# Weight loads from GpSimd's DMA queue, stores of the prepared scan features from ScalarE's

## The chip, the core and the metric

The kernel runs on one core of one Trainium2 chip. The metric is the device time of one execution in microseconds, as the median of three runs. The core has a matrix engine (PE; PEld is its weight load), three engines for elementwise work (DVE is VectorE, ACT is ScalarE, POOL is GpSimd) and SP (SyncE), which here does nothing but issue DMAs. Each engine works through its own list of instructions strictly in order, and an instruction that has to wait, a DMA issue too, holds up everything behind it in that list.

## The reference, cut to what matters

One layer of a diffusion backbone on 1024 latent and 128 context tokens (T = 1152 columns), D = 1024, all float32:

```python
h = rmsnorm(x, norm1_g) * (1 + sc1) + sh1
z = h @ w_in                                   # r, k, v, low-rank decay/rate/gate, conv branch, gates
o_a = rwkv_mixer(r, k, v, ...)                 # 16 heads, forward and backward scan over the tokens
o_b = cb * seq_conv(cc * cx, ...)
merged = g_a * (o_a @ w_pa) + g_b * (o_b @ w_pb)
x = x + gt1 * (merged @ w_o)
u = seq_conv(rmsnorm(x, norm2_g) * ... @ w_up, ...)
x = x + gt2 * ((silu(u_act) * u_lin) @ w_down)
y = rmsnorm(x, norm_f_g)
```

## The kernel before, in words

Tokens lie along the free dimension in three column blocks of 384. A *job* is one 128-row output tile of one weight matrix: 8 row blocks of the contraction, three column blocks, and three matmuls for each (the operands are split into a rounded high part and the rest, and hi·hi, hi·lo and lo·hi are summed), so 72 matmuls of 384 columns. `dense` (L230 on) is a generator over the jobs. A job's weights come as two halves of 128 x 4 x 128 values (256 KB): `load_w` (L197 on) starts the DMA into a buffer `wraw` (two buffers), `split_w` (L212 on) rounds it on ACT into `whi` and subtracts on another engine into `wlo` (three buffers each). The first half for the next job is loaded when a job begins and split after its first column block; the second half is loaded there and split later in the job. The subtraction runs on POOL while the scan is going on and on DVE afterwards. The small matrix `g2` goes through `load_w` as well, and there the matmuls read `wraw` itself.

From about 75 us to 1800 us the jobs of `w_in` and `w_pb` are interleaved with the scan, which runs as a set of generators (class `Scan`):

- `prep` (L1106 on), for each of 8 head pairs and 3 column blocks and both directions: loads `krk` and, through `lora_in`, `llo`, makes the scan features `fa` and `ak` on ACT and DVE, and stores them to DRAM (`FA`, `FB`, L1179), and once per block the bonus product `bt` to `BS` (L1167).
- `features` (L1190 on), for each of 36 scan items: loads `E`, `O` (out of `FA`) and `BK` (out of `FB`); then `prep2` makes the Gram products `gpb`, `gpk` on PE.
- `to_blocks`, `chain_load`, `chain`: the diagonal blocks go to DRAM (`Dd`) and come back as `Dm`, loaded from POOL's queue; 62 small DVE operations (`Xt`, `X`) invert them; the result is stored (`Xd`) from ACT's queue.
- `vfill`, `merge`, `scan`, `finish`: value tiles `Wt`, the scan's own matmuls, and the normalised output, which loads `fv`, `fg` and (out of `BS`) `fb`.

After 1800 us come the projections `w_pa` and `w_o`, then the feed-forward part (`w_up`, `w_down`) to the end. The program gives every operation a priority in the order in which the generators emit it; the framework makes from that, at compile time, one fixed list for each engine. Buffers that are reused put semaphore waits into those lists. Every DMA goes through one function:

```python
q = {"S": self.nc.sync, "A": self.nc.scalar, "G": self.nc.gpsimd}[QUEUE.get(kind, "S")]
q.dma_start(out=out, in_=in_)
```

`kind` is a name that the caller gives. `load_w` gives "w", the `bt` store "bs", and both feature stores "fa". The weights of the last down projection and all that has no kind go to SP.

Of the kernel before, what the change touches and what calls it, by code (L numbers as in the profile page):

```python
# [31 lines left out]

T_R, T_K, T_V, T_WD, T_AD, T_GD, T_CB, T_CC, T_CX, T_GA, T_GB = 0, 8, 16, 24, 25, 26, 27, 35, 43, 51, 59

QUEUE = dict(Xw="A", Dm="G")

PCOLS = {}
_n = 0
# [38 lines left out]
class Kern:  # L77
# [47 lines left out]
    def dma(self, out, in_, kind=None):  # L125

        q = {"S": self.nc.sync, "A": self.nc.scalar, "G": self.nc.gpsimd}[QUEUE.get(kind, "S")]
        q.dma_start(out=out, in_=in_)  # L128
# [1404 lines left out]
```

## Time and profile before

| | |
|---|---|
| median of 3 runs | 3000.38 us (2999.66 to 3003.8) |
| profiled execution | 2994.76 us, span of the profile 2993.0 us |
| PE | busy 2771.6 us, 93% of the span |
| PEld | 84% of the span |
| DVE | 2009.7 us, 67% |
| ACT | 1266.4 us, 42% |
| POOL | 318.9 us, 11% |
| DMA packets' share of 16 engines | q1 39.6%, q0 2.3%, q10 1.0% |

Busy time of PE is read as presence: matmuls overlap, and a busy PE is not one at its peak. SP has no busy time; its issues are seen in the timeline and in the view of a tile. q1 is the queue of the DMAs that SP issues, q0 that of POOL, q10 that of ACT. Where a wait is for several things, the view names what came last.

### The profile page before, as it was taken

Reading aid. Unit: us, or ns where it says so; the run is one execution under the profiler, and the core shown is the slowest. Engines: PE = TensorE matmul, PEld = TensorE weight load, DVE = VectorE, ACT = ScalarE, POOL = GpSimd, SP = SyncE. Lnnn points to the kernel's source line nnn. Section 1 sums busy time; section 2 is a strip of 40 time slices with the busy share of each in tenths; the row PEclk is TensorE's granted clock in tenths of the full one; section 3 lists DMA queues with packets and bytes.
Section 4 is the critical chain, followed back from the end, with each engine's and each line's share of the span. In section 5 each row is a group of like instructions: output and inputs, shape, how many; then the busy total and the mean of one; then the engine's idle time right before and its main releaser. Section 6 shows DMA issues by size and latency. Waiting matters only on the chain. (4 is left out here: it accounts for less than half of the span.)

```text
span 2993.0 us, 63336 instructions
## 1 busy us (share of the span) xinstructions
PE 2771.6 (93%) x24762; PEld 2514.2 (84%) x24762; DVE 2009.7 (67%) x5039; ACT 1266.4 (42%) x2540; POOL 318.9 (11%) x342
## 2 busy tenths in 40 slices
PE   7886989999989988988998999899999999999997
PEld 3774778878778877777777789899999999999996
DVE  8367666677568779989877865965555454454556
ACT  5464536454545633334543544023443241424243
POOL 3211111111111111111111112100000000000001
PEclk9997999999999999999999999999999999999999
DMA  4577646464655644544554538853211111111112
GB/s 191 179 240 204 197 121 209 145 180 143 184 172 166 197 118 127 136 115 122 148 136 120 137 101 279 291 165 98 68 43 36 50 40 45 41 41 43 41 44 81
DMA packets 425937, 388.50 MB, mean 130 GB/s; under 512 B 189477, under 2 KB 362405, under 8 KB 425637
## 3 DMA queue, kind: packets, MB, share of 16 engines
q1 hardware_dynamic: 379558, 360.84, 39.6%
q0 software_dynamic: 6912, 18.88, 2.3%
q10 hardware_dynamic: 39168, 4.73, 1.0%
q8 instruction: 195, 3.19, 0.5%
q14 instruction: 104, 0.85, 0.1%
HBM read 268.17 MB, written 116.13 MB: 128 GB/s over the span
## 5 line engine op out<-in xcount | busy, mean ns | idle before, releaser
L89 PE MATMUL psd<-h,whi 128*128 128x384 f32 x3216 | 909.3, 355 | 20.4 <-ACT h L105 9.3
L89 PEld LDWEIGHTS psd<-h,whi 128*128 128x128 f32 x3216 | 592.3, 192 | 58.6 <-issue 12.6
L89 PE MATMUL psd<-h,wlo 128*128 128x384 f32 x1608 | 564.5, 352 | 3.6 <-POOL wlo L110 3.6
L89 PE MATMUL psd<-g,whi 128*128 128x384 f32 (+1 forms) x2112 | 543.2, 338 | 0.0
L105 ACT ACTIVATE whi<-wraw 128x512 fp32r<-128x512 f32 (+2 forms) x334 | 198.4, 595 | 457.5 <-PE psd L89 358.6
L89 PEld LDWEIGHTS psd<-g,whi 128*128 128x128 f32 x2112 | 383.5, 188 | 0.3
L89 PE MATMUL psd<-g,wlo 128*128 128x384 f32 (+1 forms) x1056 | 355.9, 337 | 0.0
L110 POOL TENSOR_TENSOR wlo<-wraw,whi 128x512 fp32r<-128x512 f32 x148 | 207.1, 1402 | 1208.6 <-ACT whi L105 1057.4
L89 PEld LDWEIGHTS psd<-h,wlo 128*128 128x128 f32 x1608 | 309.3, 192 | 17.3 <-POOL wlo L110 5.2
L110 DVE TENSOR_TENSOR X<-X,Xt 128x60 f32<-128x60 f32 (+24 forms) x1116 | 258.0, 233 | 27.3
L110 DVE TENSOR_TENSOR Xt<-X,Dm 128x60 f32<-128x60 f32 (+24 forms) x1116 | 257.4, 233 | 27.0
L89 PE MATMUL psd<-a,whi 128*128 128x384 f32 x864 | 219.0, 334 | 0.0
L89 PE MATMUL psd<-x,whi 128*128 128x384 f32 x768 | 199.7, 341 | 8.0 <-ACT x L105 4.4
L89 PEld LDWEIGHTS psd<-g,wlo 128*128 128x128 f32 x1056 | 199.3, 189 | 0.0
L110 DVE TENSOR_TENSOR wlo<-wraw,whi 128x512 fp32r<-128x512 f32 (+2 forms) x186 | 113.7, 612 | 102.9 <-ACT whi L105 102.9
L89 PEld LDWEIGHTS psd<-a,whi 128*128 128x128 f32 x864 | 156.0, 188 | 0.0
L110 DVE TENSOR_TENSOR fu<-psd,rs 128x384 f32<-128x384 f32 x132 | 73.4, 556 | 117.3 <-PE psd L89 105.2
L89 PEld LDWEIGHTS psd<-x,whi 128*128 128x128 f32 x768 | 140.6, 191 | 10.3 <-ACT x L105 4.7
L89 PE MATMUL psd<-a,wlo 128*128 128x384 f32 x432 | 144.0, 334 | 0.0
L122 DVE SCALAR_TENSOR_TENSOR x<-psd,mod,x 128x384 f32<-128x384 f32 (+3 forms) x160 | 79.2, 515 | 93.9 <-PE psd L89 93.8
L105 ACT ACTIVATE BK<-BK,PC 128x128 f32<-128x128 f32 x288 | 93.2, 392 | 102.2 <-PE gpk L89 77.9
L89 PE MATMUL psd<-x,wlo 128*128 128x384 f32 x384 | 130.5, 340 | 5.4 <-DVE wlo L110 5.4
(206 smaller groups left out, 4917.7 us busy)
## 6 DMA issues: line engine op xcount, KB each, us to landing
wraw<-in_w_in SPq DMA_DIRECT2D x134, 256.0 KB, 3.2
wraw<-in_w_up SPq DMA_DIRECT2D x88, 256.0 KB, 2.6
llo<-lo SPq DMA_DIRECT2D x98, 192.0 KB, 2.7
BK<-fb SPq DMA_DIRECT2D x36, 512.0 KB, 4.8
Dm<-Dd POOLq DMA_DIRECT2D x144, 128.0 KB, 3.6
wx<-in_wmb SPq DMA_DIRECT2D x32, 512.0 KB, 5.3
fa<-fa SPq DMA_DIRECT2D x40, 384.0 KB, 2.7
fb<-ak SPq DMA_DIRECT2D x40, 384.0 KB, 3.0
```

What stands on the lines that cost most here:

```text
L89: return self.nc.tensor.matmul(out, lhsT=lhsT, rhs=rhs, start=start, stop=stop)
L105: self.nc.scalar.activation(out, in_, func, bias=bias, scale=scale)
L110: e.tensor_tensor(out, a, b, op)
L122: self.nc.vector.scalar_tensor_tensor(out, a, sc, b, op0, op1)
```

## The change

Three kinds of DMA get another issuing engine. Nothing else in the program differs.

```diff
-QUEUE = dict(Xw="A", Dm="G")
+QUEUE = dict(Xw="A", Dm="G", w="G", fa="A", bs="A")
```

So every DMA of `load_w` is issued by POOL, and every feature store of `prep` and every `bt` store by ACT. Before, SP issued all of them. They stand in the program's text where they stood; in which place they come among POOL's and ACT's instructions the framework decides.

## Rows read from the trace of the kernel before

**Rows 1.** The page: busy time by engine, and the granted clock of PE in 40 slices of 75 us.

```profile
PE 2771.6 (93%) x24762; PEld 2514.2 (84%) x24762; DVE 2009.7 (67%) x5039; ACT 1266.4 (42%) x2540; POOL 318.9 (11%) x342
...
PEclk9997999999999999999999999999999999999999
```

**Rows 2.** Busy time by stretch. Columns: stretch, its length, then for each engine busy us and (x instructions), granted clock, DMA share, GB/s.

```profile
75.00:225.00 150.00, 126.37 (x681) 115.77 (x680) 75.12 (x121) 87.99 (x178) 24.97 (x21) 0.97 0.66 210
225.00:300.00 75.00, 47.49 (x423) 31.89 (x422) 54.85 (x188) 33.74 (x81) 8.54 (x14) 0.70 0.70 204
300.00:1050.00 750.00, 688.63 (x6545) 606.32 (x6544) 514.83 (x1288) 386.21 (x830) 115.71 (x109) 0.96 0.57 172
1050.00:1800.00 750.00, 689.63 (x10373) 580.75 (x10372) 619.50 (x2202) 308.72 (x690) 106.51 (x144) 0.98 0.48 126
1800.00:1950.00 150.00, 136.69 (x755) 133.90 (x754) 120.62 (x199) 41.24 (x81) 26.89 (x17) 0.97 0.86 289
1950.00:2925.00 975.00, 974.48 (x5565) 972.51 (x5563) 515.05 (x856) 350.63 (x587) 4.35 (x4) 1.00 0.19 58
```

**Rows 3.** What PE waited for between 75 and 1800 us. Columns: who waits, for what, us in total, how many times, the longest.

```profile
PE gpb L89 <- DMA BK<-fb: 14.1, 4, 8.1
PE kps L89 <- ACT ksq L105: 9.4, 7, 2.7
PE lps L89 <- DMA llo<-lo: 8.4, 6, 2.5
PE fps L89 <- DMA fb<-bs: 7.7, 6, 2.6
PE psd L89 <- ACT gz L105: 7.5, 3, 3.5
PE gpb L89 <- DMA E<-fa: 7.4, 9, 1.9
PE psd L89 <- DMA wraw<-in_g: 6.9, 1, 6.9
...
PE psd L89 <- ACT whi L105: 5.0, 3, 3.3
...
PE psd L89 <- POOL wlo L110: 3.6, 5, 1.8
```

**Rows 4.** What SP's list of DMA issues waited for between 75 and 1800 us, the same columns.

```profile
SPq L128 <- POOL wlo L110: 124.3, 51, 7.0
SPq L128 <- DVE Xt L110: 107.6, 63, 7.0
...
SPq L128 <- DVE fa L110: 46.5, 30, 4.7
...
SPq L128 <- DVE ak L110: 31.0, 34, 3.4
...
SPq L128 <- DVE bt L110: 16.2, 13, 2.8
```

**Rows 5.** DMA issues: what, from which list, how many, KB each, median us from issue to landing.

```profile
wraw<-in_w_in SPq DMA_DIRECT2D x134, 256.0 KB, 3.2
...
Dm<-Dd POOLq DMA_DIRECT2D x144, 128.0 KB, 3.6
...
X<-in_x SPq DMA_DIRECT2D x36, 128.0 KB, 2.2
...
Xd<-X ACTq DMA_DIRECT2D x144, 32.0 KB, 2.6
```

**Rows 6.** The views of single tiles (wraw, Dm, Xd, fa, ak, bs), of each the row of one DMA: how many, ns that one issue took on its engine as min/median/max, first and last start in us.

```profile
L128 SPq DMA_DIRECT2D wraw<-in_w_in x134: 327/376/1352, 29.7 to 1787.7; - x134
...
L128 POOL DMA_DIRECT2D Dm<-Dd x144: 492/492/677, 240.5 to 1717.2; - x144
...
L128 ACTq DMA_DIRECT2D Xd<-X x144: 557/620/1862, 276.9 to 1754.0; - x144
...
L128 SPq DMA_DIRECT2D fa<-fa x56: 319/332/1653, 131.0 to 1046.7; - x56
...
L128 SPq DMA_DIRECT2D fb<-ak x56: 319/338/919, 131.8 to 1051.9; - x56
...
L128 SPq DMA_DIRECT2D bs<-bt x24: 319/332/1382, 141.0 to 1051.0; - x24
```

**Rows 7.** Timeline around the small matrix `g2`: start us, us, engine, line, operation, how many; in brackets the idle time of the engine just before and what ended it. First POOL, then SP, then PE.

```profile
198.42 1.29 POOL L110 TENSOR_TENSOR wlo<-wraw,whi 128x512 fp32r<-128x512 f32 x1 [13.89 <-ACT whi L105]
...
219.55 0.79 SPq L128 DMA_DIRECT2D fa<-fa  x2
...
221.07 0.54 SPq L128 DMA_DIRECT2D wraw<-in_g  x1
...
224.19 7.14 PE L89 MATMUL psd<-gz,wraw 128*128 128x384 f32 x14 [6.89 <-DMA wraw<-in_g]
```

**Rows 8.** What POOL waited for before it could issue a load of `Dm`, between 75 and 1800 us: us in total, times, the longest.

```profile
POOL Dm L128 <- DMA Dd<-G: 105.9, 7, 40.8
POOL Dm L128 <- DVE X L110: 94.6, 10, 23.3
POOL Dm L128 <- DVE Xt L110: 94.0, 8, 18.8
```

## The prediction

> **What bounds the kernel now.** I read the page first: PE is busy for 93% of the span and no other engine for more than 67% [rows 1], so time is won or lost only where PE stands idle. Then the busy times by stretch [rows 2]. From 1950 to 2925 us PE is busy 974.48 us of 975: nothing in the feed-forward part can be won by a queue, only lost. Idle PE lies between 75 and 1800 us: 150 − 126.37 = 23.63, 75 − 47.49 = 27.51, 750 − 688.63 = 61.37 and 750 − 689.63 = 60.37, together 172.9 us. This is the whole budget. The stretch 225 to 300 is the worst for its length, and the granted clock is 0.70 there.
>
> Then what PE waited for in that time [rows 3]. Two groups matter. Weights that came late: the load of g2 6.9 us, the rounded weights 5.0, the subtracted ones 3.6, together 15.5 us. Data that SP loads and that came last: BK 14.1, llo 8.4, fb 7.7, E 7.4, together 37.6 us in 25 waits. A third group is what ACT makes: ksq 9.4 and gz 7.5, 16.9 us. Last, SP's own list [rows 4]. A wait there is not a loss by itself, but whatever stands behind it is late. It stood for weight buffers (POOL's subtraction not done) 124.3 us in 51 waits, and for the features to be stored 46.5 + 31.0 + 16.2 = 93.7 us in 77 waits.
>
> The timeline shows what that does [rows 7]. PE waits 6.89 us for g2. Its load is issued at 221.07, directly behind feature stores and value loads, though POOL had done its last use of the weight buffers shortly after 198.42 (1.29 us).
>
> **What leaves SP.** In the scan's stretch, 134 weight loads at a median 0.376 us, 56 + 56 feature stores at 0.332 and 0.338 and 24 bonus stores at 0.332 [rows 6]: 50.4 + 18.6 + 18.9 + 8.0 = 96 us of issuing, plus the waits that stand in front of them, 124.3 + 93.7 = 218 us. 314 us of 1725, or 18% of SP's time, is no longer in front of other loads.
>
> First term, weights. The g2 load can go some 20 us earlier from POOL, so its 6.9 us should go wholly (bounds 0 and 6.9). The other 8.6 us of late weights end partly with ACT or POOL being busy; I take half, 4.3 (bounds 0 and 8.6). Together −11.2 us.
>
> Second term, the 37.6 us of data loads. If the loads were late only through their own buffers, nothing is won; if only through SP's list, all of it. SP lost 18% of its load on average, but the stores end at 1052 us and stand in the same stretch as most of these waits, so I take a third, −12.5 us (bounds 0 and −37.6).
>
> **What ACT gets.** 136 stores. ACT already issues DMAs, the stores of Xd, at a median 0.620 us each, nearly twice SP's [rows 6]: 136 x 0.62 = 84 us between 127 and 1052 us. Besides, ACT now stands where SP stood for DVE to finish a feature, up to 93.7 us if it comes there as early. Behind such a store wait the emptying of PE's result banks, the rounding of the next weights and the inputs of the next prep step. Up to 178 us of ACT's time are thus at stake, and ACT was busy 87.99 + 33.74 + 386.21 = 508 us in the 975 before 1050 [rows 2]. With the issue time and half the waits, 131 us, its load grows by 26%. PE's visible waits for ACT, 16.9 us, would grow by 4.4 at that rate; smaller rows are not in that sum, so I take +6. The bounds are 0 (every store falls into time ACT idles anyway) and +45, a quarter of the 178.
>
> **What POOL gets.** 336 loads: 134 of w_in, 2 of g2, the rest later. Now POOL issues a Dm load of 32 partitions in 0.49 us [rows 6]. A weight load covers 128 partitions, so one issue costs between 0.49 and four times that, 1.97 us. During the scan that is 67 to 268 us on an engine that is busy 319 us in all [rows 1]. There is room; a subtraction behind an issue gets later by at most 2 us, and PE waits for POOL only 3.6 us now. Landing: a 128 KB load takes 3.6 us from POOL against 2.2 from SP [rows 5], so a weight load could grow from 3.2 to 4.6 us. In the feed-forward part a job lasts 72 x 975 / 5565 = 12.6 us, a half is loaded at its start for the job after, and 1.4 us more is covered by the remaining 8; I put it at nothing there. If the cover were gone, 1.4 us on each of about 75 jobs would be 105 us.
>
> More important is the order. POOL stands for 105.9 + 94.6 + 94.0 = 294.5 us in front of Dm loads [rows 8], up to 40.8 us at once, and a weight load behind such a wait is late. SP has the like in its list already (107.6 us for the chain's Xt [rows 4], among them the load of X next to each Dm), so most of this replaces an old delay; I take +2 (bounds 0 and +15).
>
> On the transport there is a rule of the Trainium skill, SBUF — State Buffer, "Who interferes with whom": descriptors for a DMA that GpSimd issues are starved while VectorE runs in a two-port mode, and it advises a load from SP or ACT instead. It excepts tensor_tensor from those modes, and the DVE rows in [rows 4] are all of line 110, which is that operation; no run here shows the effect yet. Taken at its worst, with each scan-time load waiting for one DVE copy, it is the late-weight rival below. By the row of Dm alone the extra is 1.4 us a load and hidden.
>
> **Sum.** −11.2 − 12.5 + 6 + 2 = −15.7 us. The profiled execution took 2994.76 us, which gives 2979; the median of the runs is 5.6 us above it, so the time to be compared is 3000.38 − 15.7 = 2984.7, rounded to 2985. The lists of all engines are planned anew once DMAs change their engine, so matmuls will stand in another order; I know no sign for that and put it in the range.
>
> **Rivals.**
>
> *ACT takes the place of SP (slower).* The place is prep: a store on ACT waits for DVE's last multiply, and result banks fill up behind it. For it: the issue is dearer on ACT, and DVE is busy 514.83 of 750 us there [rows 2]. Against it: ACT idles half the time. If a quarter of the 178 us reaches PE, +45 − 23.7 + 2 = +23, 3024 us. It decides from 27.7 us, about 0.2 us a store, where my gain is eaten up (23.7 − 2 + 6 for the bound of no change).
>
> *Weights come late from POOL (slower).* A load stuck behind a Dm wait or in slow descriptor making comes after its rounding was due on ACT, and ACT blocks. The second bound of POOL, +15, and both ACT terms lead to 3000.4 − 23.7 + 15 + 20 = 3012 us; if it holds in the feed-forward part as well, up to 105 us more.
>
> *Nothing moves.* The SP waits were the data's own (buffer not free, feature not ready), so loads land when they did, and only the g2 pause goes: −6.9 + 6 + 2 = about +1, 3001 us. For it: BK, E and llo have one to three buffers and often wait for them.
>
> *More comes than I count.* SP's list runs free: all 15.5 and 37.6 us go and ACT hides its stores: −53.1 + 2, 2949 us.
>
> **Chances and range.** My case, 6 to 35 us faster: 0.47. More than that: 0.08. Nothing moves, within 6 us (0.2%, about what this kernel's measurement can tell from no change): 0.20. ACT in SP's place: 0.16. Late weights from POOL: 0.09. So faster 0.55, same 0.20, slower 0.25. The range takes in most of the first four and leaves out the dear ends on both sides, about 2 in 10: 2955 to 3014. Faster cases and slower ones share it; my own case alone is 2965 to 2994.
>
> **What would show it.** Right: PE's wait for g2 is gone and that load is issued before 210 us; the waits for BK, llo, fb and E fall from 37.6 to some 25 us; SP no longer waits for wlo before 1800 us; PE idles about 155 us instead of 173 between 75 and 1800; from 1950 to 2925 nothing changes. Each step can fail by itself: PE's waits for ACT (ksq, gz, whi, vz) above 40 us would mean that ACT took SP's place; ACT idle in front of the rounding with a weight load as its releaser, or PE below 970 us in the feed-forward stretch, that POOL's loads come late; unchanged waits for BK and E, that SP's list was never their cause. An issue of a weight load on POOL above 2 us would break my bound.

## The result, and the profile after

The changed kernel takes 3043.32 us (median, 3039.24 to 3046.97), the kernel before, measured beside it, 3001.76: a ratio of 1.0129, with a 95% interval of 1.0109 to 1.015. It is slower by 1.3%, where 2985 us was forecast; 3043 lies outside the range of 2955 to 3014.

The page after, its first line and the clock in 40 slices (now of 76 us):

```profile
PE 2786.4 (92%) x24762; PEld 2530.4 (83%) x24762; DVE 2022.8 (67%) x5039; ACT 1256.1 (41%) x2540; POOL 495.6 (16%) x678
...
PEclk9998898999899989999999999999999999999999
...
q1 hardware_dynamic: 311590, 237.61, 26.7%
q0 software_dynamic: 32000, 99.65, 10.7%
q10 hardware_dynamic: 58752, 47.20, 4.7%
```

Against [rows 1], PE is busy for 2786.4 us instead of 2771.6 with the same 24762 matmuls. The span grew by 48.2 us (2993.0 to 3041.2), so 14.8 us are PE's own time and 33.4 us are idle; the granted clock over the whole run was 0.965 after 0.972. The transfers moved as told: SP's queue fell from 39.6% to 26.7%, POOL's rose from 2.3% to 10.7%, ACT's from 1.0% to 4.7%.

Busy time by stretch, the columns as in [rows 2]; the feed-forward stretch is taken 50 us later:

```profile
75.00:225.00 150.00, 122.25 (x625) 112.22 (x625) 72.62 (x115) 80.97 (x164) 32.49 (x37) 0.93 0.59 187
225.00:300.00 75.00, 52.76 (x478) 38.47 (x478) 46.85 (x135) 37.93 (x97) 10.46 (x16) 0.86 0.73 222
300.00:1050.00 750.00, 663.77 (x6098) 588.01 (x6099) 509.39 (x1296) 354.44 (x763) 141.94 (x171) 0.94 0.53 161
1050.00:1800.00 750.00, 683.05 (x10408) 571.14 (x10407) 631.94 (x2227) 313.76 (x721) 126.53 (x187) 0.97 0.51 132
...
2000.00:2975.00 975.00, 972.60 (x5554) 970.62 (x5552) 506.42 (x835) 349.65 (x587) 100.58 (x181) 1.00 0.18 57
```

Between 75 and 1800 us PE idles 27.75 + 22.24 + 86.23 + 66.95 = 203.2 us, not 172.9. The loss is in 300 to 1050, where the stores are: 61.4 idle us became 86.2, and ACT was busy for less of it (354.44 us for 386.21), so it was not overloaded. The granted clock there is 0.94 after 0.96, and 0.93 after 0.97 in the stretch ahead: means of the two levels, 1.2 and 2.4 GHz, with more time at the lower, after more pauses of PE. The feed-forward stretch is as it was (972.60 of 975).

What PE waited for between 75 and 1800 us, the columns as in [rows 3]:

```profile
PE lps L89 <- DMA llo<-lo: 14.0, 11, 4.6
PE gpb L89 <- DMA BK<-fb: 10.9, 4, 6.2
PE kps L89 <- ACT ksq L105: 10.6, 7, 4.6
PE gpb L89 <- DMA E<-fa: 10.4, 11, 1.8
PE psd L89 <- ACT whi L105: 8.4, 3, 4.5
...
PE fps L89 <- DMA fb<-bs: 6.2, 3, 3.5
PE mps L89 <- ACT ak L105: 5.6, 3, 3.2
PE psd L89 <- ACT gz L105: 5.2, 3, 4.3
PE vps L100 <- ACT vz L105: 5.0, 3, 2.1
PE lps L89 <- ACT ak L105: 4.7, 3, 3.2
...
PE psd L89 <- POOL wlo L110: 1.4, 3, 0.7
```

The wait for the load of `g2`, 6.9 us in [rows 3], is gone. The four data loads stand at 14.0 + 10.9 + 10.4 + 6.2 = 41.5 us for 37.6. Many small waits for ACT are new or have grown (`ak`, `whi`, `vz`, `fb`, `RSt` and others). Summed by the engine that ended them, all rows of this view give 52.4 us for ACT before and 82.4 after; DVE 53.1 and 62.3; DMA 52.6 and 43.4. So +30.0 for ACT, +9.2 for DVE, −9.2 for DMA: the waits that grew most are those for ACT, and what DVE added, the DMAs gave back.

Where ACT stood more than before is in the views of the tiles `ak` and `fa`: what their instructions waited for (total us, times). First `ak`, before and after:

```profile
  DMA fb<-ak: 5.6, 6
```

```profile
  DMA fb<-ak: 40.6, 22
```

These 40.6 us are ACT's, which writes `ak`: it stood until the store of the previous `ak` (there is one buffer) had landed. Then `fa`, before and after:

```profile
  ACT e L105: 7.1, 10
```

```profile
  ACT e L105: 45.0, 19
```

Here DVE stood in front of the product `fa`, 45.0 us for ACT's exponential. Moreover ACT idled 20.6 + 22.8 + 16.4 = 59.8 us directly in front of the stores of FA, FB and BS (its gaps ahead of these 136 issues, added up from the trace). That is a ring: ACT waits for DVE's product, stores it, waits for the landing, and DVE then waits for what ACT makes next. The experiments show how much of it comes with the new issuer and how much with the new lists.

### The profile page after: what moved, and what is told of

Read it like the earlier page. It is cut to its first block, busy times and chain, and to the rows that moved or that the text cites. A ratio compares the mean times of both kernels' runs of the same rounds, so it can differ in the third digit from the quotient of the medians.

```text
span 3041.2 us, 63326 instructions
## 1 busy us (share of the span) xinstructions
PE 2786.4 (92%) x24762; PEld 2530.4 (83%) x24762; DVE 2022.8 (67%) x5039; ACT 1256.1 (41%) x2540; POOL 495.6 (16%) x678
## 3 DMA queue, kind: packets, MB, share of 16 engines
q1 hardware_dynamic: 311590, 237.61, 26.7%
q0 software_dynamic: 32000, 99.65, 10.7%
## 5 line engine op out<-in xcount | busy, mean ns | idle before, releaser
L89 PEld LDWEIGHTS psd<-h,whi 128*128 128x128 f32 x3216 | 601.1, 195 | 62.3 <-issue 12.4
L110 POOL TENSOR_TENSOR wlo<-wraw,whi 128x512 fp32r<-128x512 f32 x148 | 200.9, 1358 | 1191.5 <-ACT whi L105 1127.8
L110 DVE TENSOR_TENSOR X<-X,Xt 128x60 f32<-128x60 f32 (+24 forms) x1116 | 260.6, 236 | 26.7
```

Source lines behind the costliest of these rows:

```text
L89: return self.nc.tensor.matmul(out, lhsT=lhsT, rhs=rhs, start=start, stop=stop)
L110: e.tensor_tensor(out, a, b, op)
```

## The experiments

**One half at a time.** Lists planned by the framework, as in every kernel here unless said otherwise.

```diff
-QUEUE = dict(Xw="A", Dm="G")
+QUEUE = dict(Xw="A", Dm="G", w="G")              # w_only
+QUEUE = dict(Xw="A", Dm="G", fa="A", bs="A")     # stores_only
```

> Only the weight loads go to POOL; the stores stay with SP. Theory ACT (the stores on ACT cost the 41 us): 2985 to 3000 us. Theory POOL (weight loads from POOL cost them): 3030 to 3045. Theory plan (a changed queue makes the framework write other lists for all engines, and the lists of the changed kernel are worse): nothing follows for this one, its lists are new again; anything from 2990 to 3045.

Measured: 2984.86 us, ratio 0.9956 [0.9938, 0.9974].

> Only the feature and bonus stores go to ACT; the weight loads stay with SP. Theory ACT: 3030 to 3045 us, with ACT's wait for the store of ak near the 40.6 us of the changed kernel. Theory POOL: 2990 to 3005. Theory plan: its lists are new as well; anything from 2990 to 3045.

Measured: 3039.65 us, 1.0136 [1.0106, 1.0166]. The two halves have opposite signs: the weight loads on POOL win 13 us, the stores on ACT lose 41. PE's waits of the two kernels, first the weight loads' (late weights alone), then the stores':

```profile
PE psd L89 <- POOL wlo L110: 0.9, 1, 0.9
...
PE lps L89 <- ACT whi L105: 0.6, 1, 0.6
```

```profile
PE kps L89 <- ACT ksq L105: 12.0, 7, 4.2
PE gpb L89 <- DMA BK<-fb: 11.3, 3, 5.8
PE psd L89 <- ACT cct L105: 9.7, 1, 9.7
PE psd L89 <- ACT whi L105: 9.4, 4, 4.3
PE vps L100 <- ACT vz L105: 7.6, 5, 2.3
PE lps L89 <- DMA llo<-lo: 6.6, 7, 2.8
...
PE gpb L89 <- DMA E<-fa: 5.9, 8, 1.4
...
PE fps L89 <- DMA fb<-bs: 4.3, 2, 2.8
```

With the weight loads alone, late weights fall from 15.5 us to 1.5 (PE's waits for the rounding of the scan's own low-rank weights, `lwhi`, whose loads stay with SP, rise from 3.0 to 8.1). With the stores alone the four data loads do fall, from 37.6 to 28.1 us, and all waits for ACT rise from 52.4 to 95.0; the longest of these, 9.7 us, can be followed in ACT's timeline of the same kernel (columns as in [rows 7]):

```profile
656.71 0.33 ACTq L128 DMA_DIRECT2D fa<-fa  x1
657.07 1.28 ACT L105 ACT_TABLE_LOAD   x1 [1.39 <-DVE fa L110]
658.36 0.47 ACT L105 ACTIVATE fb<-fps,gneps 128x256 f32<-128x256 f32 x1
659.47 0.33 ACTq L128 DMA_DIRECT2D bs<-bt  x1
660.34 0.33 ACTq L128 DMA_DIRECT2D fb<-ak  x1
660.71 0.45 ACT L105 ACTIVATE fps<-fps,gneps 128x256 f32<-128x256 f32 x1 [1.88 <-DVE ak L110]
661.09 0.97 ACT L105 ACTIVATE BK<-BK,PC 128x128 f32<-128x128 f32 x3
664.77 0.63 ACT L105 ACTIVATE lwhi<-lwraw 128x512 fp32r<-128x512 f32 x1 [2.71 <-DMA lwraw<-in_lw]
665.30 1.55 ACT L105 ACTIVATE BK<-BK,PC 128x128 f32<-128x128 f32 x5
666.76 0.47 ACT L105 ACTIVATE cct<-psd 128x384 f32<-128x384 f32 x1
```

PE stands from 657.6 us for a result bank that the last line empties. In front of it in ACT's list are three stores, each waiting for DVE (1.39 and 1.88 us are shown), and after them a load that came late. Nothing in that stretch is long; ACT is simply not there when the bank is full. ACT's wait for the landing of `ak`, expected near 40.6 us, is 31.5 in this kernel.

**The issue alone.** 136 more stores from ACT whose data are always ready (128 x 32 values), each behind one of the real stores' places; all lists held as in the kernel before, by a chain of order-only dependences for each engine:

```diff
+def keep_order(tc):
...
+            tc.add_manual_dep(i, p.name, mybir.DependencyInfo(mybir.DependencyClass.NoSync,
+                              mybir.DependencyReason.DATA), reason="keep_order")
...
+                i = nc.scalar.dma_start(out=EX[:, 32 * j:32 * j + 32], in_=ident[:, 0:32])
```

> The kernel before with its own lists and queues, and 136 more DMAs on ACT, each of 128 x 32 numbers from a constant that is ready, right behind the place of one feature or bonus store. They cost ACT the issue and wait for nothing. Theory issue time (ACT's sequencer is held about 0.4 to 0.6 us by each): 3020 to 3035 us. Theory waits (ACT is held because the store's data or its buffer is not ready): 2997 to 3008.

Measured: 3006.57 us against 3006.33, 1.0004 [0.9986, 1.0023]. Issuing as such costs nothing that can be measured here. The run is also the control for the runs that follow: holding the order costs nothing either.

**Lists against queues.** Each change of an engine makes the framework plan all lists anew (in the traces of the two kernels, PE's differ at 14499 of 24762 places). So the order was held, with the same `keep_order`: the lists of before with each of the changes, and the lists of after with the queues of before.

> The three kinds of DMA are issued by POOL and ACT as in the changed kernel, but every engine keeps the order that its list had in the kernel before (the moved DMAs stand in POOL's and ACT's lists where they came in the overall order of that plan). Theory plan: the queues as such cost nothing, 2985 to 3003 us. Theories ACT and POOL: the cost lies in who issues, 3025 to 3045.

Measured: 3032.12 us, 1.0112 [1.0082, 1.0142], where theories ACT and POOL had it.

> SP issues all three kinds again as in the kernel before, but every engine keeps the order that its list has in the changed kernel (the DMAs stand in SP's list where they came in the overall order of that plan). Theory plan: 3035 to 3060 us, the lists carry the loss and SP has its old load on top. Theories ACT and POOL: 2995 to 3010, since the queues are those of before.

Measured: 3075.46 us, 1.026 [1.0218, 1.0303], above both ranges. No feature store is on ACT here, and yet both waits of the ring are longer than in the changed kernel (the views of `ak` and `fa`):

```profile
  DMA fb<-ak: 69.1, 25
```

```profile
  ACT e L105: 61.0, 17
```

> The order of every list as in the kernel before; only the weight loads go to POOL. Theory ACT (the stores on ACT cost the time, whatever the lists): 2980 to 2997 us, about as much won as with the framework's own lists (2984.9). Theory list luck (that gain came from other lists, POOL's loads bring nothing): 2995 to 3010.

Measured: 3022.19 us, 1.0045 [1.0025, 1.0064], outside both ranges.

> The order of every list as in the kernel before; only the feature and bonus stores go to ACT. Theory ACT: 3035 to 3050 us, the old-list cost of both (35 us) plus what the weight loads win. Theory list luck: 3000 to 3015.

Measured: 3015.61 us, 1.0035 [1.0017, 1.0053], far below the range of theory ACT and at the upper end of the other. ACT's wait in the view of `ak`:

```profile
  DMA fb<-ak: 12.4, 9
```

> The order of every list as in the kernel before; the stores go to POOL instead of ACT, the weight loads stay with SP. Theory ACT (what stands behind a store on ACT is urgent, POOL's list is nearly empty): 2975 to 3000 us. Theory store (a store issued anywhere but from SP lands later, and the single buffers of fa and ak come free later): 3020 to 3045.

```diff
+QUEUE = dict(Xw="A", Dm="G", fa="G", bs="G")
```

Measured: 3026.21 us, 1.0055 [1.0032, 1.0078]. Theory ACT missed this one as well; theory store had it.

Every pairing of a list with queues for which it was not planned is slower than before, the weight loads too, which win with lists of their own. But it is not so that a list fits only its own queues. With all stores on ACT the order of before (1.0035) is faster than the order that the framework planned for these queues (1.0136), and with all three changes the two orders are level (1.0112 and 1.0129, with intervals that overlap); together the changes cost some 34 us in the old order, more than the 13.5 and 11 of the two parts. So of the 41 us of stores_only some 11 come with the engine in an unchanged order, and the other 30 with the lists that were planned for it. What the order changes can be seen in the traces: in the old order ACT idles 21.4 us in front of the stores instead of 57.2, it waits 12.4 us for the landing of `ak` instead of 31.5, and PE waits 64.2 us for ACT instead of 95.0. newlist_oldqueue has 88.1 us of PE's waits for ACT, with no such store on ACT: those lists carry the waits themselves.

**How much lists scatter.** One constant of the program's own clock model, which only shifts the order in which the generators emit:

```diff
-        s.use("A", 100 + 0.84 * fsize(out))
+        s.use("A", 104 + 0.84 * fsize(out))
```

> The queues of the kernel before; in the program's own model one ACT operation counts 104 ns plus its columns instead of 100. No operation changes, but the order of emission and with it every list does. Theory scatter (any new set of lists moves the time by tens of us, and the two single changes drew a good and a bad one): 2975 to 3035 us, off the kernel before by more than 10 us. Theory fit (lists planned for their queues are about equally good): 2990 to 3010.

Measured: 2985.27 us, 0.9947 [0.9926, 0.9968].

> The same shake of the lists with the queues of the changed kernel. Theory scatter: anything from 2985 to 3060 us, no closer to 3043 than the shaken kernel before is to 3000. Theory fit: 3030 to 3055.

Measured: 3040.69 us, 1.0144 [1.0113, 1.0175].

> The same shake, only the weight loads on POOL. Theory scatter: 2975 to 3035 us, the gain of 12 us may be gone. Theory fit: 2980 to 2995.

Measured: 2973.65 us, 0.9923 [0.99, 0.9945].

> The same shake, only the stores on ACT. Theory scatter: 2990 to 3060 us. Theory fit: 3030 to 3050.

Measured: 3027.63 us, 1.0097 [1.0071, 1.0124]. A change that means nothing moves the kernel by 16 us; but against the shaken kernel before, the stores still cost 42 us and the weight loads still win 12. The signs are not luck of one plan. The ranges of theory fit held for shaken1_after alone: shaken1_before, shaken1_w and shaken1_stores came out below theirs, shaken1_w below that of theory scatter too.

**Which wait, which store, which engine.** First, the stores emitted one step of the generator later, after DVE's last product (once from ACT, once from SP as control):

```diff
-                for dst, src in (("FA", FAo), ("FB", B)):
...
             yield
+            if d:
+                K.dma(dr["BS"][p][:, t0:t0 + TH], bt, "bs")
+            for a, b in segs:
...
+                for dst, src in (("FA", FAo), ("FB", B)):
```

> Before's queues but the feature and bonus stores from ACT, as in stores_only; the generator of prep emits them one step later, after the step in which DVE makes the last product, so that they get a later priority in ACT's list; all lists planned afresh. If ACT's wait for DVE's product in front of the stores is what costs (57 us of ACT's idle time stand there in stores_only), that idle time falls below 30 us and the ratio from 1.0136 to at most 1.006. If the landing of the store before the one ak buffer is written again is what costs, ACT's wait for it (31.5 us in stores_only) stays or grows and the ratio stays at 1.010 or more. If neither wait matters and it is the lists, the idle time falls and the ratio stays at 1.010 or more.

Measured: 3044.95 us, 1.0132 [1.0095, 1.017].

> Control: the same later emission, but stores from SP as in the kernel before. Every theory: within 0.994 to 1.006, the scatter of lists planned afresh (the shaken kernel before came to 0.995). Above that, emitting later would have a cost of its own that the run with ACT has to be read against.

Measured: 3000.14 us, 0.999 [0.9968, 1.0012]. The pair did not separate what it should, because the framework put the stores back to nearly the same places: in the traces, against stores_only, ACT's list differs at 31 of 2820 places and PE's at 21 of 24762, and ACT's idle time in front of the stores stayed at 58.2 us. The control has the lists of the kernel before (ACT's at every place), so its 0.999 is a second reading of one plan. A second `ak` buffer, which would take the landing out of the ring, was not tried.

Then single kinds, with a `kind` of their own for FA and FB, and all three kinds on POOL:

```diff
+QUEUE = dict(Xw="A", Dm="G", FB="A")             # fb_on_act
+QUEUE = dict(Xw="A", Dm="G", FA="A")             # fa_on_act
+QUEUE = dict(Xw="A", Dm="G", FA="A", bs="A")     # fabs_on_act
+QUEUE = dict(Xw="A", Dm="G", fa="G", bs="G")     # own_stores_pool
```

> Before's queues, and only the 56 stores of ak to FB from ACT; FA and BS stay with SP; lists planned afresh. These are the stores whose landing ACT itself waits for before it writes the one ak buffer again. If that loop is the cause, this run has most of the cost of stores_only: 1.009 or more, and ACT's wait for the landing is 25 us or more. If the cost goes by the number of stores or by the idle time in front of them (25 of 57 us), it is 1.003 to 1.008. If the lists alone decide, any value between 0.994 and 1.014.

Measured: 2986.41 us, 0.9946 [0.9924, 0.9968].

> Before's queues, and all 136 stores from POOL instead of ACT, lists planned afresh. If the cost of stores_only is ACT's own time (POOL has no result banks to empty and no rounding of weights to do), this is within 0.994 to 1.006. If moving the stores off SP costs wherever they go, because the new lists are worse or the stores start later, it is 1.010 or more. In before's lists POOL cost 1.0055 against 1.0035 on ACT.

Measured: 2999.93 us, 0.9985 [0.9963, 1.0007].

> Only the 56 stores to FA from ACT; FB and BS from SP; lists planned afresh. If FA is the dear one, 1.008 or more; if BS is (its store stands in front of the features, and ACT's idle time before one is 0.6 us against 0.3 us before one of FA in stores_only), at most 1.005 while the run with FA and BS is above 1.009. If it takes all kinds together, 0.994 to 1.006.

Measured: 2987.96 us, 0.9956 [0.9942, 0.9969].

> The complement of fb_on_act: FA and BS (56 + 24 stores) from ACT, FB from SP; weights from SP; lists planned afresh. If one of these two kinds is what costs on ACT, the ratio is 1.009 or more, as in stores_only. If it takes all three kinds together (each alone hides in ACT's idle time), it is 0.994 to 1.006, as fb_on_act was.

Measured: 2963.17 us, 0.9882 [0.9863, 0.9901], below every range that was given, faster than both kernels and the fastest of all. POOL's own waits in own_stores_pool, the columns as in [rows 8]:

```profile
POOL fa L128 <- DVE fa L110: 148.6, 35, 10.5
POOL fb L128 <- DVE ak L110: 83.0, 26, 9.3
...
POOL bs L128 <- DVE bt L110: 35.9, 11, 10.7
```

With lists of their own, 267.5 us of standing in front of the same stores cost nothing measurable on POOL, and on ACT 57 us stand in a kernel that loses 41. With the order held, POOL is no better than ACT (1.0055 and 1.0035, with intervals that overlap), so this is not yet a difference of the engines. The landing of FB alone is not it either: with FB on ACT, ACT still stands 30.4 us for it, and the kernel is no slower. All kernels with lists of their own, by the kinds that ACT issues; idle time of ACT directly in front of the stores and PE's waits for ACT and for DMAs between 75 and 1800 us, added up from the trace:

| kernel | stores on ACT | ratio | ACT idle before them | PE waits for ACT | PE waits for DMA |
|---|---|---|---|---|---|
| before | none | 1 | – | 52.4 | 52.6 |
| shaken1_before | none | 0.9947 | – | 54.5 | 53.3 |
| late_stores_sp | none | 0.999 | – | 54.6 | 53.5 |
| own_stores_pool | none (POOL) | 0.9985 | – | 52.6 | 47.6 |
| w_only | none | 0.9956 | – | 48.9 | 43.7 |
| shaken1_w | none | 0.9923 | – | 52.6 | 41.9 |
| fabs_on_act | FA, BS | 0.9882 | 20.8 | 48.3 | 45.7 |
| fb_on_act | FB | 0.9946 | 31.4 | 57.4 | 48.2 |
| fa_on_act | FA | 0.9956 | 37.3 | 53.7 | 54.3 |
| shaken1_after | all | 1.0144 | 51.4 | 79.9 | 38.6 |
| shaken1_stores | all | 1.0097 | 55.1 | 75.8 | 34.2 |
| stores_only | all | 1.0136 | 57.2 | 95.0 | 29.5 |
| late_stores_act | all | 1.0132 | 58.2 | 86.1 | 33.4 |
| after | all | 1.0129 | 59.8 | 82.4 | 43.4 |

Among these kernels there are two groups with nothing between: up to two of the kinds on ACT, 48 to 57 us of PE's waits for ACT and no loss; all three, 76 to 95 us and 1.0 to 1.4% more, in four plans (late_stores_act has nearly the lists of stores_only). In the second group ACT comes later for PE each time; where the weights stay with SP (three of its rows), the transfers come earlier (29.5 to 34.2 us). With the order held there is something between: all stores on ACT, 64.2 us and 0.35%.

What is shown is that the loss comes with the stores, that it stands in PE's waits for ACT, and that with the stores alone moved most of it belongs to the order that was planned for them. Why the framework's order with all three kinds on ACT is so much worse than with two is open. A ring that closes only when ACT waits for DVE before every store and for the landing after the last fits the table, but newlist_oldqueue has the ring without a store on ACT, and fb_on_act stands 31.4 us in front of its stores and 30.4 us for the landing at no loss. With one plan tried, part of the 1.2% of fabs_on_act can be such luck as the 0.5% of the shaken kernel before.

## Why the prediction was wrong

**The budget** was right: between 75 and 1800 us is where the time moved, and the feed-forward part stayed (972.60 of 975).

**Late weights (−11.2).** Right in direction and half in size. The load of `g2` is issued at 208.21 us (221.07 in [rows 7]) and its wait is gone:

```profile
206.23 1.69 POOL L110 TENSOR_TENSOR wlo<-wraw,whi 128x512 fp32r<-128x512 f32 x1 [1.24 <-ACT whi L105]
208.21 0.55 POOL L128 DMA_DIRECT2D wraw<-in_g  x1 [0.30 <-POOL wlo L110]
```

But PE reaches these matmuls only at 240.01 us instead of 224.19, and with the stores alone moved SP issues the same load at 202.42 us: the new lists do as much here as the queue. With the weight loads alone the late weights lost 15.5 − 1.5 = 14.0 us, near the bound of 15.5, and w_only won 13. In the changed kernel the waits for rounded weights are 9.0 us (5.0 before), so with 1.4 for the subtracted ones 10.4 of the 15.5 are left: −5.1 instead of −11.2.

**POOL (+2).** No cost is seen: PE waits 4.1 us for POOL instead of 4.9. The bound of 2 us for an issue held by far. The weight loads in the view of the tile `wraw` after, columns as in [rows 6]:

```profile
L128 POOL DMA_DIRECT2D wraw<-in_w_in x134: 536/556/701, 1.4 to 1839.1; - x134
L128 POOL DMA_DIRECT2D wraw<-in_w_up x88: 536/536/545, 2160.5 to 2941.1; - x88
```

A weight load lands after 3.5 us instead of 3.2, not 4.6. By the Trainium skill, SBUF — State Buffer, "Who interferes with whom", such loads could have been starved while DVE runs in a two-port mode, from which that section excepts tensor_tensor. The trace agrees with the exception: between 75 and 1800 us 3220 of DVE's 3769 instructions are tensor_tensor, and a load landed 0.3 us later. The rival of late weights from POOL did not happen; the 20 us that it puts down for ACT come from no row and no other term.

**Data loads (−12.5).** The mechanism was right, the size about right for what it stood for: −9.5 us with the stores alone, −3.7 with the weight loads alone (33.9). In the changed kernel it was gone, 41.5 for 37.6: `llo` rose by 5.6 and E by 3.0. `llo` is not stored by `prep` at all, and with the stores alone on ACT both fell, so late stores do not explain it; what does is open.

**ACT (+6).** This step failed. I grew the two groups of waits that I had listed, 16.9 us, by ACT's load of 26%. All rows in which PE waits for ACT make 52.4 us, so I scaled a third of them; and scaling was the wrong working, since ACT had half its time free and lost none of it to issuing (1.0004 with 136 more issues, 0.327 us each for the real ones instead of the 0.62 I took from Xd). What grew was the time at which ACT is late for someone: PE's waits for it rose by 30.0 us (after) and 42.6 us (stores_only), where I had 6. The upper bound of +45, a quarter of the 178 us, holds both, but its quarter was a guess, and that it holds is luck. The rival "ACT takes the place of SP", at 3024 us and a chance of 0.16, has the right sign and place. Its mechanism, a store on ACT that waits for DVE while a result bank fills, is seen in the timeline of stores_only; but in an unchanged order the stores on ACT cost only some 11 us, so the mechanism does not account for most of the loss. The rival was 19 us too low and had all of the 23.7 us of gains beside it. Its sign, four waits above 40 us, was too narrow: ksq, gz, whi and vz make 29.8 us (10.6 + 5.2 + 9.0 + 5.0), the rest is spread over some twenty rows. Nor was there a term for PE's own time, 14.8 us of the longer span, or for its waits for DVE, 9.2.

**The lists.** I wrote that they would change and that I knew no sign, and put them at nothing. That failed too: a constant that means nothing is worth 16 us, and most of the 41 us of the stores (all but 11) came with the lists made for them. A chance for "nothing moves, within 6 us" of 0.20 was too much: of eleven other plans in the table one came within 0.2% of the kernel before.

## What to carry to other kernels

A DMA moved to another engine is not priced by its issue, which cost nothing measurable here, but by the waits in front of it, by what stands behind it, and by the lists that a planner makes for it. Count all rows in which the bottleneck waits for that engine, not the two largest, before scaling anything. When a planner makes the lists, change the parts of an edit one by one, measure the scatter of a change that means nothing, and try the old order with the new queues: here two of the three kinds of stores on ACT won 1.2%, all three lost 1.4%, and the same three in the old order lost 0.35%.

## What was not expected of the hardware

An issue from ACT was no dearer than from SP for the same store, and the shape counted for more: from ACT 0.327 us for a feature store (0.332 from SP) beside 0.62 for Xd. From POOL the same weight load took 0.536 to 0.556 us for 0.376 from SP, and hardly more than a `Dm` load of 32 partitions, 0.492. The stores landed later when they left SP: FA 3.7 us after the issue for 2.7, FB 4.0 for 3.0 (medians of the two kernels), which is part of ACT's 40.6 us; but from POOL it was 3.6 and 3.9 at no loss. By the Trainium skill, DMA: Bandwidth & Descriptors, "Rules for kernel authors", spreading DMAs over engines only saves issue time; here the issue time saved was worth little, and the places in the engines' lists were worth more.
